# One sum of a seven-product group made by an accumulating DMA and used last, two more such groups per layer, and earlier chained sums, in a two-layer block on one Trainium2 core

## The chip, the cores and the metric

The kernel runs on one core of a Trainium2 chip. The metric is the device time of one execution in microseconds. The kernel before took 2232.99 us, the median of three runs (2231.83, 2232.99, 2235.12).

## What is computed

Two layers of a decoder act on 256 tokens of width 2048, in 32-bit floats. Each layer is a token mixer and then a SwiGLU feed-forward part; a last RMS norm follows.

```python
h = h + mixer(rmsnorm(h, w_mix))        # layer 0: gated delta rule and RG-LRU; layer 1: two attentions
h = h + swiglu(rmsnorm(h, ffn_norm[layer]), ffn_w_gate[layer], ffn_w_up[layer], ffn_w_down[layer])

def swiglu(hn, w_gate, w_up, w_down):
    return (jax.nn.silu(hn @ w_gate) * (hn @ w_up)) @ w_down
```

The gate and up matrices are 2048 x 5632, the down matrix is 5632 x 2048. The change lies in the feed-forward part, in the first weight products of layer 0, and in the last norm.

## The kernel before

**Split numbers.** A product in full float precision is made of three products of rounded numbers. A tile x is split into `hi`, x rounded to the matmul's format (a copy on ACT), and `lo` = x - hi (a subtraction on DVE). Then x·w is hi·hi + hi·lo + lo·hi: three matmuls. The activations X and hid lie in SBUF split already. Each weight tile of 128 x 1024 (512 KB) is loaded by SP's DMA queue into a `raw` buffer (`load`, L166; three buffers of one pool and four of another in the feed-forward part), and split by `split` (L176) into `whi` (four buffers) and `wlo` (three).

**Plain units.** A unit is one weight tile: two slices of 128 rows by 512 columns. It is multiplied with both halves of the tokens (t = 0, 1): 2 x 2 x 3 = 12 matmuls of 512 columns, into two of four PSUM banks F[t][i] (`Bank.add`, L399).

**Groups by sevens.** Four units (two row pairs u, two column blocks i) and the two token halves make a 2 x 2 by 2 x 2 block product. `seven` (L424) makes it of seven block products instead of eight, in Winograd's form of Strassen's scheme. Four sums of weight tiles are needed: T1 = b11 + b12, T2 = T1 + b22, T3 = b12 + b22, T4 = T2 + b21, whose signs are taken into the activations' sums and the results. `total` (L372) makes one sum on DVE into a `T` tile (three buffers) and splits it into the pair `thi` (ACT) and `tlo` (DVE), of which there are two buffers each. The sums of activations are made ahead by `combine` (L382), once per group of four X or hid slices, on DVE and ACT. A group has seven steps of six matmuls. Four products go to banks M[0] to M[3], the others straight to F; `ends` (L449) joins the M banks into four tiles e at the end. In order, the steps of the kernel before are: 1 b11; 2 T1; 3 b22; 4 T3; 5 T2; 6 b21; 7 T4.

**Blocks.** `block` (L409) runs the plain units of a block and puts the steps of its groups between them: the number of steps made after unit j grows by `len(sevens) / gaps`. In a block with 8 plain units and two groups (14 steps), three steps follow unit 1, four follow unit 2, three unit 3 and four unit 4: steps 4 to 7 of each group stand together. In a block with one group a plain unit stands between steps 5 and 6.

**The feed-forward part** (`ffn`, L482) goes through 11 gate blocks of 512 columns in pieces of 4, 4 and 3. A gate block is 16 units for X: four groups of four. `groups` says how many of these go by sevens: none in the first, two in each other. After each piece two down blocks (p = 0, 1) multiply the piece's hid with the rows of the down matrix. A down block after four gate blocks has four groups of four units, one of them by sevens. `hooks` are calls ahead of unit j: `turn` transposes the last block's results into hid, `late` combines hid[:, 0:4].

**Order.** The framework plans the order of each engine's instructions ahead of time. It takes what is ready by its own times, in the order of the program, so an engine's order can differ from that of the code. Each engine then works its list off in order, and waits for semaphores. A buffer of a tag is given again when its last reader is done.

**First products and last norm.** `first` (L210) loads the tokens and the first weights of layer 0 slice by slice and splits them, for u < 2 slice by slice, then two slices at a time. `second_half` (L1137) makes the last norm: per half of the rows two means (L1145), a root on ACT (L1147), a reciprocal, and the scalings (`ready`, L1155).

Of the kernel before, what the change touches and what calls it, by code (L numbers as in the profile page):

```python
# [4 lines left out]
F32, F32R, I32 = dt.float32, dt.float32r, dt.int32  # L5
AF = mybir.ActivationFunctionType
ALU = mybir.AluOpType
# [3 lines left out]
D = 2048  # L11
T = 256
NK = D // 128
# [34 lines left out]
def body(tc, A, out):  # L48
# [161 lines left out]
    def first(src, n, w):  # L210

        m = T + n * 128
        xw = [h.rearrange("p a b -> p (a b)")] + [ogp.tile([128, 4 * D // 2], F32, name=f"xw{i}", tag="og") for i in range(3)]
        xw = [t[:, 0:4 * m].rearrange("p (k n) -> p k n", n=m) for t in xw]
        Ps = [acc.tile([128, T], F32, name="Pw", tag="acc") for _ in range(n)]
        for a, b in [(k, k + 1) for k in range(4)] + [(k, k + 2) for k in range(4, NK, 2)]:
            nc.sync.dma_start(xw[a // 4][:, a % 4:a % 4 + b - a], src[:, a:b])  # L220
            if b == 12:
                nc.sync.dma_start(tab[:, 0:NTAB0], A["tab"][:, 0:NTAB0])
                nc.sync.dma_start(col[:, 16:], A["col"][:, 16:])
        for u in range(NK // 2):
            hi = wh.tile([128, 1024], F32R, name="whi")
            lo = wl.tile([128, 1024], F32R, name="wlo")
            for a, b in [(0, 1), (1, 2)] if u < 2 else [(0, 2)]:
                ks = range(2 * u + a, 2 * u + b)
                for k in ks:
                    x = xw[k // 4][:, k % 4, 0:T]  # L230
                    S.activation(X[:, k, 0], x, AF.Copy, scale=w[:, k:k + 1])
                    V.scalar_tensor_tensor(out=X[:, k, 1], in0=x, scalar=w[:, k:k + 1], in1=X[:, k, 0].bitcast(F32),
                                           op0=ALU.mult, op1=ALU.subtract)
                raw = xw[u // 2][:, u % 2 * 2 + a:u % 2 * 2 + b, T:]
                c = slice(512 * a, 512 * b)
                rows = lambda t: t[:, c].rearrange("p (k n) -> p k n", n=n * 128)
                if u == a == 0:
                    V.tensor_copy(rows(hi), raw)
                else:
                    S.copy(rows(hi), raw)  # L240
                V.tensor_sub(rows(lo), raw, rows(hi).bitcast(F32))
                for k in ks:
                    for i, P in enumerate(Ps):
                        ws = slice((k % 2 * n + i) * 128, (k % 2 * n + i + 1) * 128)
                        PE.matmul(P, hi[:, ws], X[:, k, 0], start=k == 0, stop=False)
                        PE.matmul(P, hi[:, ws], X[:, k, 1], start=False, stop=False)
                        PE.matmul(P, lo[:, ws], X[:, k, 0], start=False, stop=k == NK - 1)
            if u % 2:
                sq = xw[u // 2][:, :, 0:T]
                tc.keep_in_program_order(S.activation(sq, sq, AF.Square))  # L250
        return Ps, [t[:, :, 0:T] for t in xw]
# [60 lines left out]

    def sumsq(g, *ts):
        for t in ts or range(2):
            j = (mx.tile([128, 1024], F32, name="junk", tag="T", bufs=3)[:, 0:512] if more else
                 mx.tile([128, 512], F32, name="junk", tag="t2", bufs=4))
            S.activation(j, h[:, t, g * 512:(g + 1) * 512], AF.Square, accum_out=ssp[:, t, g:g + 1])

# [50 lines left out]
        return f  # L369


    def total(a, b, name):  # L372

        t = mx.tile([128, 1024], F32, name=name, tag="T", bufs=3)
        V.tensor_tensor(out=t, in0=a, in1=b, op=ALU.add)  # L375
        hi = fp.tile([128, 1024], F32R, name="thi", tag="thi", bufs=2)
        lo = fp.tile([128, 1024], F32R, name="tlo", tag="tlo", bufs=2)
        S.copy(hi, t)  # L378
        V.tensor_sub(lo, t, hi.bitcast(F32))  # L379
        return t, (hi, lo)  # L380

    def combine(x4):  # L382

        f = mx.tile([128, 4, T], F32, name="cf", tag="T", bufs=3)
        c = mx.tile([128, 4, 2, 128], F32, name="cc4", tag="T", bufs=3)
        r = fp.tile([128, 2, 4, 2, 128], F32R, name="comb", tag="comb", bufs=3)
        V.tensor_tensor(out=f, in0=x4[:, :, 0].bitcast(F32), in1=x4[:, :, 1].bitcast(F32), op=ALU.add)
        a11, a21, a12, a22 = (f[:, 2 * j:2 * j + 2, t * 128:(t + 1) * 128] for j in range(2) for t in range(2))
        for i, (x, y) in enumerate(((a21, a22), (a21, a11), (a22, c[:, 1]), (a12, c[:, 2]))):
            V.tensor_tensor(out=c[:, i], in0=x, in1=y, op=ALU.subtract)  # L390
        S.copy(r[:, 0], c)
        V.tensor_tensor(out=r[:, 1], in0=c, in1=r[:, 0].bitcast(F32), op=ALU.subtract)
        return r

    class Bank:
# [3 lines left out]
        def add(self, A, B):  # L399
# [6 lines left out]
                PE.matmul(self.t, xl, hi[:, kk], start=False, stop=kk == 1 and self.i == self.n - 1)  # L406
            self.i += 1

    def block(src, x, comb, nd, hooks, tail=0, lead=2, trail=None):  # L409


# [12 lines left out]
        def seven(m):  # L424
# [2 lines left out]
            q = lambda j, t: lambda kk: xs(4 * m + 2 * j + kk, t)  # L427
            b11 = load(src(0, 2 * m))
            M[0].add(q(0, 0), split(b11))
            yield  # L430
            b12 = load(src(1, 2 * m))
            t, w = total(b11, b12, "T1")
            M[1].add(cx(0), w)
            yield
            b22 = load(src(1, 2 * m + 1))
            F[0][1].add(cx(3), split(b22))
            yield
            M[3].add(cx(1), total(b12, b22, "T3")[1])
            yield
            t, w = total(t, b22, "T2")  # L440
            M[2].add(cx(2), w)
            yield
            b21 = load(src(0, 2 * m + 1))
            F[0][0].add(q(1, 0), split(b21))
            yield
            F[1][0].add(q(1, 1), total(t, b21, "T4")[1])
            yield

        def ends():  # L449
            c1, v, w5, w7 = (mx.tile([128, 512], F32, name=f"e{i}", tag=f"e{i}", bufs=1) for i in range(4))  # L450
            S.copy(c1, M[0].t)
            for o, a, b, op in ((v, M[2], c1, ALU.subtract), (w5, M[1], v, ALU.add), (v, M[3], v, ALU.add), (w7, M[3], w5, ALU.add)):
                V.tensor_tensor(out=o, in0=a.t, in1=b, op=op)
            return [[c1, w5], [v, w7]]
# [27 lines left out]
    def ffn(L, then, fin=None):  # L482
# [18 lines left out]
        for groups in ((0, 2, 2, 2), (2, 2, 2, 2), (2, 2, 2)):  # L501
# [3 lines left out]
            for j in range(piece):  # L505
# [3 lines left out]
                    hooks[8] = rstd  # L509
                    hooks[10] = lambda: cx.update({1: combine(X[:, 4:8])})  # L510
                if j == 1 and piece == 3:
                    hooks.update(late)
                F, e = block(lambda i, u: gu[b, u, i], lambda k: X[:, k], {m: lambda m=m: cx[m] for m in range(groups[j])}, 4, hooks)
                a = [fp.tile([128, 512], F32, name=f"fa{t}", tag="fa", bufs=2) for t in range(2)]
                for t in range(2):
                    if e:
                        V.tensor_tensor(out=a[t], in0=F[t][0], in1=e[t][0], op=(ALU.add, ALU.subtract)[t])
                    S.activation(a[t], a[t] if e else F[t][0], AF.Silu, scale=nrm["rs"][:, t:t + 1])
                for t in range(2):
                    if e:  # L520
                        V.tensor_tensor(out=e[t][1], in0=F[t][1], in1=e[t][1], op=ALU.add)
                    V.scalar_tensor_tensor(out=a[t], in0=e[t][1] if e else F[t][1], scalar=nrm["rs"][:, t:t + 1], in1=a[t],
                                           op0=ALU.mult, op1=ALU.mult)
                    todo.append((hid, j, t, a[t]))
                b += 1
            u0 = 2 * (b - piece)
            for p in range(2):
                end = b == NB and p == 1
                hooks = {2: turn} if todo else {}
                if p == 0 and piece == 4:  # L530
                    hooks.update(late)
                if end and fin:
                    hooks.update({5: lambda: then(0), 6: lambda: then(1)})
                last = (3, 1, 3) if end and fin else (0, 5 if 4 in hooks else 2)
                F, e = block(lambda i, u: dn[2 * p + i, u0 + u], lambda k: hid[:, k], {0: lambda: ch[0]}, piece, hooks, *last)
                hs = [[h[:, t, (2 * p + i) * 512:(2 * p + i + 1) * 512] for i in range(2)] for t in range(2)]
                for t in range(2):
                    for i in range(2):
# [598 lines left out]
    def second_half(add):  # L1137

        o = fo[0]
        x, y, z = ([f[:, t:t + 1] for t in range(2)] for f in (xf, yf, zf))  # L1140

        def root(t):

            for i, o in ((2, z[t]), (3, x[t])):
                V.scalar_tensor_tensor(out=o, in0=ssp[:, t, i:i + 1], scalar=1.0 / D, in1=part[:, t:t + 1] if i == 2 else z[t],  # L1145
                                       op0=ALU.mult, op1=ALU.add)
            S.activation(y[t], ssp[:, t, 3:4], AF.Sqrt, scale=1.0 / D, bias=z[t])  # L1147

        def rate(t):
# [15 lines left out]
        add(0, 1)  # L1165
        sumsq(3, 0)
        add(1, 0)
        root(0)
        sumsq(2, 1)
        rate(0)  # L1170
        ready(0, 0)
        add(1, 1)
        sumsq(3, 1)
        ready(0, 2)
        ready(0, 3)
        root(1)
        ready(0, 1)
        rate(1)
        for g in (0, 2, 1, 3):
# [97 lines left out]
```

## Time and profile before

| | before |
|---|---|
| median of three runs | 2232.99 us |
| the profiled execution's own time | 2232.51 us |
| its span, first to last instruction | 2230.7 us |
| matmuls recorded | 11026 |
| granted TensorE clock, mean | 0.999 |
| read from HBM | 418.22 MB |

PE is the engine of the matmuls, PEld its weight loads, DVE the vector engine, ACT the scalar engine, POOL the general one, SP the one that issues most DMAs; a name with q is an engine's queue. A line of a group gives line, engine, operation, the tile written and those read, shapes, count, then busy us and the mean ns of one, then the idle time before them and what ended it. A line in order of time begins with the start and the duration in us. A line of waits gives the total, the number and the longest. A line of a stretch gives for PE, PEld, DVE, ACT and POOL the busy us and the count, then the granted clock, the share of the 16 DMA engines and GB/s. Matmuls overlap, so the time of one is read from the distance of starts.

### The profile page before, as it was taken

How to read it: one execution, taken by the hardware profiler on the slowest of the kernel's cores; microseconds unless marked ns; L12 is line 12 of the kernel's file. 1: busy time of each engine (PE TensorE's matmuls, PEld its weight loads, DVE VectorE, ACT ScalarE, POOL GpSimd, SP SyncE). 2: the span in 40 equal slices, each digit the busy share in tenths (PEclk: the TensorE clock that was granted, in tenths of full speed). 3: DMA queues.
4: the chain of work that ended last, by engine and by line, in shares of the span. 5: the costliest groups of instructions: out<-in, count | busy, mean ns of one | idle time of the engine just before them, and what ended most of it. 6: DMA issues, size and time to landing. Idle time of an engine off the chain costs nothing.

```text
span 2230.7 us, 30096 instructions
## 1 busy us (share of the span) xinstructions
PE 2215.9 (99%) x11026; PEld 1852.0 (83%) x11026; DVE 1928.9 (86%) x2716; ACT 1278.9 (57%) x1670; POOL 2.1 (0%) x6
## 2 busy tenths in 40 slices
PE   9999999999999999999999999999999999999998
PEld 8888888888888888888878888888888888888886
DVE  8899676789989999899966658857999999999998
ACT  6776664565555665565654444445665466555565
POOL 0000000000000000000000000000000000000000
PEclk9999999999999999999999999999999999999999
DMA  7445445665565666656545455456665666666563
GB/s 280 161 144 168 140 150 187 214 208 195 192 215 196 201 195 203 207 187 200 180 158 175 158 172 172 162 186 217 208 198 191 208 205 203 194 210 202 181 219 131
DMA packets 117780, 422.29 MB, mean 189 GB/s; under 512 B 13152, under 2 KB 14688, under 8 KB 117504
## 3 DMA queue, kind: packets, MB, share of 16 engines
q1 hardware_dynamic: 117344, 420.10, 56.7%
q8 instruction: 86, 1.41, 0.2%
q14 instruction: 62, 0.51, 0.1%
q10 hardware_dynamic: 288, 0.27, 0.0%
HBM read 418.22 MB, written 2.10 MB: 188 GB/s over the span
## 4 chain that ended last, share of the span: by engine, by line
PE 97%; DVE 1%; DMA 1%; ACT 0%; issue 0%; SPq 0%; DVEq 0%; ACTq 0%
PE F L405 16%; PE F L406 16%; PE F L404 16%; PE Pw L199 11%; PE Pw L204 6%; PE Px L303 5%; PE Px L305 5%; PE Px L304 5%; PE M L404 4%; PE M L405 4%; PE M L406 4%; PE Ph L492 1%; PE Psc L1053 1%; PE Pt L326 0%; PE Ps L563 0%; DMA raw<-in_gu 0%
## 5 line engine op out<-in xcount | busy, mean ns | idle before, releaser
L179 ACT CAST whi<-raw 128x1024 fp32r<-128x1024 f32 x724 | 760.7, 1052 | 744.8 <-PE F L406 359.1
L180 DVE TENSOR_TENSOR wlo<-raw,whi 128x1024 fp32r<-128x1024 f32 x724 | 876.5, 1219 | 185.0 <-PE Px L304 74.0
L199 PE MATMUL Pw<-X,whi 128*128 128x512 f32 x1088 | 388.0, 400 | 0.0
L404 PE MATMUL F<-whi,X 128*128 128x512 f32 x848 | 330.5, 391 | 0.0
L405 PE MATMUL F<-wlo,X 128*128 128x512 f32 x848 | 330.4, 390 | 0.0
L406 PE MATMUL F<-whi,X 128*128 128x512 f32 x848 | 330.1, 389 | 0.0
L204 PE MATMUL Pw<-X,wlo 128*128 128x256 f32 x1088 | 304.7, 280 | 0.1
L378 ACT CAST thi<-T 128x1024 fp32r<-128x1024 f32 x208 | 219.1, 1054 | 98.6 <-DVE T L375 71.5
L379 DVE TENSOR_TENSOR tlo<-T,thi 128x1024 fp32r<-128x1024 f32 x208 | 252.5, 1219 | 24.7 <-ACT thi L378 24.2
L199 PEld LDWEIGHTS Pw<-X,whi 128*128 128x128 f32 x1088 | 204.1, 188 | 47.4 <-issue 0.5
L405 PE MATMUL F<-wlo,hid 128*128 128x512 f32 x536 | 208.9, 390 | 0.0
L406 PE MATMUL F<-whi,hid 128*128 128x512 f32 x536 | 208.7, 389 | 0.0
L404 PE MATMUL F<-whi,hid 128*128 128x512 f32 x536 | 208.6, 390 | 0.0
L204 PEld LDWEIGHTS Pw<-X,wlo 128*128 128x128 f32 x1088 | 205.4, 189 | 1.2 <-DVE wlo L180 0.7
L406 PEld LDWEIGHTS F<-whi,X 128*128 128x128 f32 x848 | 159.2, 188 | 33.1
L404 PEld LDWEIGHTS F<-whi,X 128*128 128x128 f32 x848 | 159.2, 188 | 32.7
L405 PEld LDWEIGHTS F<-wlo,X 128*128 128x128 f32 x848 | 159.3, 188 | 32.5
L375 DVE TENSOR_TENSOR T<-raw,raw 128x1024 f32<-128x1024 f32 x98 | 119.2, 1218 | 11.0 <-DMA raw<-in_gu 8.9
L375 DVE TENSOR_TENSOR T<-T,raw 128x1024 f32<-128x1024 f32 x104 | 126.6, 1218 | 1.9 <-DMA raw<-in_dn 1.7
L404 PE MATMUL M<-thi,comb 128*128 128x512 f32 x312 | 121.3, 391 | 0.6 <-ACT thi L378 0.6
L405 PE MATMUL M<-tlo,comb 128*128 128x512 f32 x312 | 121.6, 390 | 0.0
L406 PE MATMUL M<-thi,comb 128*128 128x512 f32 x312 | 121.5, 389 | 0.0
(385 smaller groups left out, 3217.1 us busy)
## 6 DMA issues: line engine op xcount, KB each, us to landing
raw<-in_gu SPq DMA_DIRECT2D x352, 512.0 KB, 4.1
raw<-in_dn SPq DMA_DIRECT2D x176, 512.0 KB, 4.3
raw<-in_w0w SPq DMA_DIRECT2D x72, 512.0 KB, 3.6
raw<-in_wo SPq DMA_DIRECT2D x64, 512.0 KB, 3.5
raw<-in_w1w SPq DMA_DIRECT2D x64, 512.0 KB, 3.6
raw<-in_w1x SPq DMA_DIRECT2D x32, 512.0 KB, 3.6
raw<-in_w0x SPq DMA_DIRECT2D x16, 512.0 KB, 3.6
xw<-in_xw SPq DMA_DIRECT2D x6, 768.0 KB, 10.9
```

The source lines that it names most:

```text
L179: S.copy(hi, raw)
L180: V.tensor_sub(lo, raw, hi.bitcast(F32))
L199: PE.matmul(P.rearrange("p a b -> p (a b)"), hi[:, kk], X[:, k].rearrange("p a b -> p (a b)"), start=k == 0, stop=False)
L204: PE.matmul(P[:, 0], lo[:, kk], X[:, k, 0], start=False, stop=k == NK - 1)
L303: PE.matmul(Ps[t], x[:, 0, ts], hi[:, kk], start=k == 0, stop=False)
L304: PE.matmul(Ps[t], x[:, 0, ts], lo[:, kk], start=False, stop=False)
L375: V.tensor_tensor(out=t, in0=a, in1=b, op=ALU.add)
L378: S.copy(hi, t)
L379: V.tensor_sub(lo, t, hi.bitcast(F32))
L404: PE.matmul(self.t, xh, hi[:, kk], start=self.i == kk == 0, stop=False)
L405: PE.matmul(self.t, xh, lo[:, kk], start=False, stop=False)
L406: PE.matmul(self.t, xl, hi[:, kk], start=False, stop=kk == 1 and self.i == self.n - 1)
```

## The change

- In `seven`, T3 is no longer made on DVE: once T1 has been summed, POOL issues a DMA that loads b22 a second time and adds it onto b12 in SBUF. T3 is used last. The order of steps is now: 1 b11; 2 b22; 3 T1; 4 b21; 5 T2; 6 T4; 7 T3.
- T1, T2 and T4 are made in one tile, in place, each right behind the split of the sum before it, a step ahead of its own split. `total` becomes `halves`, which only splits. The tag `T` has two buffers in place of three.
- In the down blocks p = 1 of pieces with four gate blocks, hid's second group of four goes by sevens too; its `combine` is made ahead of unit 9 of the down block p = 0. `comb` has four buffers in place of three.
- The tiles e take the place of the tiles `fa` in the gate blocks.
- In the third piece, `late` is called ahead of unit 6 of its second block and no longer ahead of unit 4.
- In `first`, slices 4 and 5 are loaded and split one by one.
- In `second_half`, the two means are made in calls of their own: the first stands ahead of the scalings of the other half, the second behind the root.

```diff
-        for a, b in [(k, k + 1) for k in range(4)] + [(k, k + 2) for k in range(4, NK, 2)]:
+        for a, b in [(k, k + 1) for k in range(6)] + [(k, k + 2) for k in range(6, NK, 2)]:
...
-            for a, b in [(0, 1), (1, 2)] if u < 2 else [(0, 2)]:
+            for a, b in [(0, 1), (1, 2)] if u < 3 else [(0, 2)]:
...
-    def total(a, b, name):
-
-        t = mx.tile([128, 1024], F32, name=name, tag="T", bufs=3)
-        V.tensor_tensor(out=t, in0=a, in1=b, op=ALU.add)
+    def halves(t):
+
         hi = fp.tile([128, 1024], F32R, name="thi", tag="thi", bufs=2)
         lo = fp.tile([128, 1024], F32R, name="tlo", tag="tlo", bufs=2)
         S.copy(hi, t)
         V.tensor_sub(lo, t, hi.bitcast(F32))
-        return t, (hi, lo)
+        return hi, lo
...
-        r = fp.tile([128, 2, 4, 2, 128], F32R, name="comb", tag="comb", bufs=3)
+        r = fp.tile([128, 2, 4, 2, 128], F32R, name="comb", tag="comb", bufs=4)
...
             b11 = load(src(0, 2 * m))
             M[0].add(q(0, 0), split(b11))
-            yield
             b12 = load(src(1, 2 * m))
-            t, w = total(b11, b12, "T1")
-            M[1].add(cx(0), w)
+
+            t = mx.tile([128, 1024], F32, name="T", tag="T", bufs=2)
+            more_of = lambda a, b: V.tensor_tensor(out=t, in0=a, in1=b, op=ALU.add)
+            more_of(b11, b12)
+
+            G.dma_start(b12, src(1, 2 * m + 1), accum_op=ALU.add)
             yield
             b22 = load(src(1, 2 * m + 1))
             F[0][1].add(cx(3), split(b22))
             yield
-            M[3].add(cx(1), total(b12, b22, "T3")[1])
-            yield
-            t, w = total(t, b22, "T2")
-            M[2].add(cx(2), w)
+            M[1].add(cx(0), halves(t))
+            more_of(t, b22)
             yield
             b21 = load(src(0, 2 * m + 1))
             F[0][0].add(q(1, 0), split(b21))
             yield
-            F[1][0].add(q(1, 1), total(t, b21, "T4")[1])
+            M[2].add(cx(2), halves(t))
+            more_of(t, b21)
+            yield
+            F[1][0].add(q(1, 1), halves(t))
+            yield
+            M[3].add(cx(1), halves(b12))
             yield
...
-                    hooks.update(late)
+
+                    hooks[6] = late[4]
...
+                    hooks[9] = lambda hid=hid: ch.update({1: combine(hid[:, 4:8])})
...
-                F, e = block(lambda i, u: dn[2 * p + i, u0 + u], lambda k: hid[:, k], {0: lambda: ch[0]}, piece, hooks, *last)
+                F, e = block(lambda i, u: dn[2 * p + i, u0 + u], lambda k: hid[:, k],
+                             {m: lambda m=m: ch[m] for m in range(1 + (p == 1 and piece == 4))}, piece, hooks, *last)
...
+        def mean(t, i):
+
+            V.scalar_tensor_tensor(out=(z, x)[i][t], in0=ssp[:, t, 2 + i:3 + i], scalar=1.0 / D,
+                                   in1=z[t] if i else part[:, t:t + 1], op0=ALU.mult, op1=ALU.add)
+
         def root(t):
...
-            for i, o in ((2, z[t]), (3, x[t])):
-                V.scalar_tensor_tensor(out=o, in0=ssp[:, t, i:i + 1], scalar=1.0 / D, in1=part[:, t:t + 1] if i == 2 else z[t],
-                                       op0=ALU.mult, op1=ALU.add)
```

More of the change, by code (lines that the diff above doesn't have):

```diff
@@ L314, in sumsq @@
         for t in ts or range(2):
-            j = (mx.tile([128, 1024], F32, name="junk", tag="T", bufs=3)[:, 0:512] if more else
+            j = (mx.tile([128, 1024], F32, name="junk", tag="T", bufs=2)[:, 0:512] if more else
                  mx.tile([128, 512], F32, name="junk", tag="t2", bufs=4))
@@ L379, in total @@
         V.tensor_sub(lo, t, hi.bitcast(F32))
-        return t, (hi, lo)
+        return hi, lo
     def combine(x4):
-        f = mx.tile([128, 4, T], F32, name="cf", tag="T", bufs=3)
-        c = mx.tile([128, 4, 2, 128], F32, name="cc4", tag="T", bufs=3)
-        r = fp.tile([128, 2, 4, 2, 128], F32R, name="comb", tag="comb", bufs=3)
+        f = mx.tile([128, 4, T], F32, name="cf", tag="T", bufs=2)
+        c = mx.tile([128, 4, 2, 128], F32, name="cc4", tag="T", bufs=2)
+        r = fp.tile([128, 2, 4, 2, 128], F32R, name="comb", tag="comb", bufs=4)
         V.tensor_tensor(out=f, in0=x4[:, :, 0].bitcast(F32), in1=x4[:, :, 1].bitcast(F32), op=ALU.add)
@@ L407, in add, with sums @@
             self.i += 1
+    def sums():
+        return [[mx.tile([128, 512], F32, name=f"e{t}{i}", tag=f"e{t}{i}", bufs=1) for i in range(2)] for t in range(2)]
     def block(src, x, comb, nd, hooks, tail=0, lead=2, trail=None):
@@ L445, in seven @@
             yield
-            F[1][0].add(q(1, 1), total(t, b21, "T4")[1])
+            M[2].add(cx(2), halves(t))
[4 more added lines that the diff above has]
+            M[3].add(cx(1), halves(b12))
             yield
         def ends():
-            c1, v, w5, w7 = (mx.tile([128, 512], F32, name=f"e{i}", tag=f"e{i}", bufs=1) for i in range(4))
+            (c1, w5), (v, w7) = sums()
             S.copy(c1, M[0].t)
@@ L511, in ffn @@
                 if j == 1 and piece == 3:
-                    hooks.update(late)
+                    hooks[6] = late[4]
                 F, e = block(lambda i, u: gu[b, u, i], lambda k: X[:, k], {m: lambda m=m: cx[m] for m in range(groups[j])}, 4, hooks)
-                a = [fp.tile([128, 512], F32, name=f"fa{t}", tag="fa", bufs=2) for t in range(2)]
+                a = e or sums()
                 for t in range(2):
                     if e:
-                        V.tensor_tensor(out=a[t], in0=F[t][0], in1=e[t][0], op=(ALU.add, ALU.subtract)[t])
-                    S.activation(a[t], a[t] if e else F[t][0], AF.Silu, scale=nrm["rs"][:, t:t + 1])
+                        V.tensor_tensor(out=a[t][0], in0=F[t][0], in1=e[t][0], op=(ALU.add, ALU.subtract)[t])
+                    S.activation(a[t][0], a[t][0] if e else F[t][0], AF.Silu, scale=nrm["rs"][:, t:t + 1])
                 for t in range(2):
                     if e:
[L521 to L524, printed above, removed]
+                        V.tensor_tensor(out=a[t][1], in0=F[t][1], in1=e[t][1], op=ALU.add)
+                    V.scalar_tensor_tensor(out=a[t][0], in0=a[t][1] if e else F[t][1], scalar=nrm["rs"][:, t:t + 1],
+                                           in1=a[t][0], op0=ALU.mult, op1=ALU.mult)
+                    todo.append((hid, j, t, a[t][0]))
                 b += 1
@@ L1167, in second_half @@
         add(1, 0)
+        mean(0, 0)
         root(0)
+        mean(0, 1)
         sumsq(2, 1)
@@ L1173, in second_half @@
         sumsq(3, 1)
+        mean(1, 0)
         ready(0, 2)
@@ L1176, in second_half @@
         root(1)
+        mean(1, 1)
         ready(0, 1)
```

## The prediction

> **What bounds the kernel now.** I read the page's head and chain first, then PE's waits, then the groups, one feed-forward stretch in time order, and last the DMA rows.
>
> ```profile
> span 2230.7 us, 30096 instructions
> ...
> PE 2215.9 (99%) x11026; PEld 1852.0 (83%) x11026; DVE 1928.9 (86%) x2716; ACT 1278.9 (57%) x1670; POOL 2.1 (0%) x6
> ...
> PE 97%; DVE 1%; DMA 1%; ACT 0%; issue 0%; SPq 0%; DVEq 0%; ACTq 0%
> ```
> ```profile
> PE Pz L93 <- ACT tab L90: 2.7, 1, 2.7
> PE Pw L245 <- ACT whi L240: 0.7, 1, 0.7
> PE Pgate L645 <- ACT cx L582: 0.6, 1, 0.6
> PE M L404 <- ACT thi L378: 0.6, 1, 0.6
> PE F L405 <- DVE tlo L379: 0.4, 1, 0.4
> ```
> The chain that ended last is PE, and all of PE's listed waits come to 5.0 us, 1.0 of it in the feed-forward parts. So time is worth what matmuls are worth, as long as nobody makes PE wait. What a matmul is worth is not the 390 ns that its row shows, because matmuls overlap; it is the distance between starts:
>
> ```profile
> 699.71 0.39 PE L404 MATMUL M<-thi,comb 128*128 128x512 f32 x1
> ...
> 701.07 0.39 PE L404 MATMUL F<-whi,X 128*128 128x512 f32 x1
> ...
> 702.43 0.39 PE L404 MATMUL F<-thi,X 128*128 128x512 f32 x1
> 702.66 0.39 PE L405 MATMUL F<-tlo,X 128*128 128x512 f32 x1
> ...
> 703.79 0.39 PE L404 MATMUL F<-whi,X 128*128 128x512 f32 x1
> ...
> 706.51 0.39 PE L404 MATMUL M<-whi,X 128*128 128x512 f32 x1
> ```
> These are steps 5, 6 and 7 of a group by sevens, then a plain unit. Six matmuls take 1.36 us, so one takes 0.227, and twelve 2.72. The second engine is nearly as full:
>
> ```profile
> 510.00:552.00 42.00, 42.00 (x190) 34.60 (x189) 41.60 (x43) 25.52 (x27) 0.00 (x0) 1.00 0.59 201
> ```
> In this 42-us stretch (one gate block) DVE is busy 41.6 us (the column after PE's and PEld's), ACT 25.5, the DMA engines 0.59, at full PE clock.
>
> **Part 1, two more groups by sevens per stage.** A plain group of four tiles is 48 matmuls, a group by sevens 42.
>
> ```profile
> L404 PE MATMUL M<-thi,comb 128*128 128x512 f32 x312 | 121.3, 391 | 0.6 <-ACT thi L378 0.6
> L378 ACT CAST thi<-T 128x1024 fp32r<-128x1024 f32 x208 | 219.1, 1054 | 98.6 <-DVE T L375 71.5 <-PE M L406 23.6 <-PE F L406 1.8
> ```
> 312 at six per group, or 208 sums at four, make 52 groups. The edit adds one in the p = 1 down block of each of the two four-block pieces of each of two layers: 4 groups, 24 matmuls, 24 x 0.227 = **-5.4 us**. PE does these inside its bound, so it counts in full if DVE follows.
>
> **Part 2, DVE.** Successive 1.22-us operations on DVE start 1.14 apart (702.26 and 703.40 below). Each group loses one of four sums: a gate block has two groups and falls by 2.3 of its 41.6 us. The changed down block goes from 23 large operations to 28 (8 units, twice 10): 28 x 1.14 + 12 small at 0.61 (717.14 to 717.75) = 39.2, under PE's 180 x 0.227 = 40.9. The block ahead of it gets one more `combine`:
>
> ```profile
> L390 DVE TENSOR_TENSOR cc<-cf,cc 128x256 f32<-128x256 f32 x20 | 8.3, 417 | 0.0
> L392 DVE TENSOR_TENSOR comb<-cc,comb 128x1024 fp32r<-128x1024 f32 x10 | 12.2, 1220 | 0.3
> ```
> ```profile
> 485.18 0.87 PE Ph L492 x8
> ```
> ```profile
> 717.14 0.68 DVE L453 TENSOR_TENSOR e<-M,e 128x512 f32<-128x512 f32 x1
> 717.75 1.22 DVE L180 TENSOR_TENSOR wlo<-raw,whi 128x1024 fp32r<-128x1024 f32 x1
> ```
> Its sum is as large as the last row's: 1.22 + 4 x 0.42 + 1.22 = 4.1 us. There 22 x 1.14 + 2 x 4.1 + 14 x 0.61 = 41.8 stands against PE's 186 x 0.227 + 0.9 of transposes = 43.1 (the 0.87 is the row of Ph). Hidden by 1.3 us; were that cover gone, each us would land on PE four times. Cost 0. ACT, at 25.5 of 42, gets three casts more per new group and has room. The new POOL transfer waits for DVE's first sum alone, and nothing else is queued on POOL (2.1 us in all).
>
> **Part 3, the sum that DMA makes.** b12 += b22 leaves DVE for an accumulating transfer that POOL issues, 56 in all; no row shows one. Its nearest row is a plain load of the same 512 KB:
>
> ```profile
> q1 hardware_dynamic: 117344, 420.10, 56.7%
> raw<-in_gu SPq DMA_DIRECT2D x352, 512.0 KB, 4.1
> ACT whi L179 <- DMA raw<-in_gu: 16.7, 8, 4.5
> 675.65 1.22 DVE L375 TENSOR_TENSOR T<-raw,raw 128x1024 f32<-128x1024 f32 x1
> ```
> Landing takes 4.1 us; I bound the new one by 4.1 and by twice that. It has far more: the last row is the first sum of the group whose steps 5 to 7 are shown above. DVE ended it at 676.9, the transfer may go then, and its split has to be there for step 7, not before step 5 ends at 701.07 (Part 4). That is 24 us of cover; past it every us would cost each group a us. Engine time: 0.567 x 2230.7 us for 420.10 MB is 1.58 us per load; two transfers per 41.7-us block (180 x 0.227 and 0.9 of transposes) at 1.58 to 3.16 raise the share from 0.59 to 0.67 or 0.74. They'd fill the engines only at (1 - 0.59) x 41.7 / 2 = 8.5 us each. The raw buffers stay seven, and one of them is held longer; but with 352 gate loads issued a cast waited for one only 8 times, 16.7 us in all and none of it in PE's list, so I take 0. The Trainium skill ("Collectives: The Full Stack", The bandwidth ceiling) says that an add in the DMA engine costs because it reads two sources, not because it adds. By it the estimate is the 3.16 end, and the sum stays.
>
> **Part 4, three pairs in a row.** This is the step I distrust. The split pairs `thi`/`tlo` have two buffers. Before, a group uses them in steps 2, 4, 5, 7; now in 3, 5, 6, 7. So step 7's pair takes step 5's buffer, with only step 6 between. What that chain lasts is in step 7's pair before, which took step 4's:
>
> ```profile
> 699.91 1.05 ACT L378 CAST thi<-T 128x1024 fp32r<-128x1024 f32 x1 [0.30 <-PE M L406]
> 701.00 1.23 DVE L379 TENSOR_TENSOR tlo<-T,thi 128x1024 fp32r<-128x1024 f32 x1 [0.81 <-ACT thi L378]
> 702.26 1.23 DVE L375 TENSOR_TENSOR T<-T,raw 128x1024 f32<-128x1024 f32 x1
> 703.40 1.22 DVE L379 TENSOR_TENSOR tlo<-T,thi 128x1024 fp32r<-128x1024 f32 x1
> ```
> Step 4 ended at 699.71, `tlo` at 702.23: 2.52 us, and PE wanted it at 702.66, two steps and one matmul later (2.95). With one step between, PE wants it after 1.36 + 0.23 = 1.59: late by 0.93, with the handover (0.05) 0.98 us. Steps 4 to 7 stand together, without a plain unit between, in all groups of blocks with two groups: 40 gate + 8 down = 48. Price if PE keeps the order: 48 x 0.98 = +47 us. But the planner doesn't keep it where an operand is late:
>
> ```profile
> 1038.73 0.50 PE L404 MATMUL F<-thi,X 128*128 128x512 f32 x1
> 1039.07 0.40 PE L405 MATMUL F<-wlo,X 128*128 128x512 f32 x1
> ...
> 1041.40 0.39 PE L405 MATMUL F<-tlo,X 128*128 128x512 f32 x1
> ```
> Here step 7's first matmul runs, its `tlo` isn't there, and matmuls of the next plain unit fill 2.3 us before step 7 goes on. The next unit (2.72 us, ready long before) covers 0.98 easily. What is left is the seam: 1038.73 to 1039.07 is 0.34 instead of 0.23, a gap of 0.11. Bounds: 0 to 48 x 0.11 = 5.3; below zero isn't possible, as nothing here removes work. Most seams of such stretches have none, so I take one in five: **+1.1**.
>
> **Part 5, the chained sums one step ahead.** ACT's 71.5 us of waiting for DVE's T (row of L378) shrink, but ACT isn't the bound. Of PE's two feed-forward waits, 0.4 for `tlo` and 0.6 for `thi`, I take the first, whose engine gets room: **-0.4** (bounds 0 and -1.0).
>
> **Part 6, start and end.** The third weight pair is now split by halves.
>
> ```profile
> 12.12 0.38 PE L245 MATMUL Pw<-X,whi 128*128 128x256 f32 x1 [0.65 <-ACT whi L240]
> ...
> 13.05 0.28 PE L246 MATMUL Pw<-X,whi 128*128 128x256 f32 x1
> 13.38 0.74 PE L247 MATMUL Pw<-X,wlo 128*128 128x256 f32 x4
> ```
> PE waited 0.65 for the whole cast, then 13.38 - 13.05 - 0.12 = 0.21 for the difference; half-size operations come early enough for both: **-0.9**, bounds 0 (a later DVE wait takes it back) and -1.1. At the end the first mean of the second row block goes ahead of two scalings:
>
> ```profile
> 2223.34 0.29 ACT L1147 ACTIVATE fin<-ssp,fin 128x1 f32<-128x1 f32 x1 [0.73 <-DVE fin L1145]
> 2223.67 0.16 DVE L1151 RECIPROCAL fin<-fin 128x1 f32<-128x1 f32 x1 [0.15 <-ACT fin L1147]
> ```
> The root no longer waits 0.73, but DVE still has the two scalings and the other mean: **-0.2** (0 to -0.3).
>
> **Sum.** -5.4 + 1.1 - 0.4 - 0.9 - 0.2 = -5.8. The profiled execution took 2232.5 us (the span and 1.8 around it), 0.5 under the median of the three runs. 2232.5 - 5.8 = **2226.7 us**, or 0.26% less. A measurement of this kernel can tell about 0.2%, 4.5 us, from no change.
>
> **Rivals.**
> *Seams everywhere* (0.17): every step 7 pays its 0.11, +4.2 on the forecast: 2230.9, no change. For it: `thi` is ready 1.3 us after step 5, step 6 lasts 1.36, so just in time. Against: most filled steps show none.
> *Step 7 waits* (0.10, slower): PE keeps the order and Part 4's +47 less 1.1 gives 2272.6. It decides from 6.9 / 48 = 0.14 us of wait per group, which eats all the gain. For it: 2.52 against 1.59. Against: the fill at 1038.73.
> *The transfer is dear* (0.10, slower): at 10 us of all engines each, a block of 16 loads needs 25.3 + 20 = 45.3 us instead of 41.7; 28 such blocks give +101, 2328; from 8.5 on it costs. Against: a load takes 1.58.
> *POOL and DVE get in each other's way* (0.05): if each issue holds DVE for one operation, 1.22, a block gets 2.4 back of the 2.3 it gained, and the changed down blocks, with 1.7 spare, lose 0.7 each: 2230 to 2237. The Trainium skill ("SBUF — State Buffer", Who interferes with whom) has a DVE instruction with two SBUF inputs contend with GpSimd's reads; no run here shows it yet.
> *Forecast* (0.58), its own range 2223 to 2229.5.
>
> Range: 2222.5 to 2237 leaves out the two slower rivals, 0.20. Faster by over 0.2% (under 2228.5): nearly all of the forecast, 0.54. Within: the first and last rival and the forecast's edge, 0.25. Slower: 0.21.
>
> **What would show it.** 24 fewer matmuls; 56 issues on POOL landing within 10 us; on PE's rows the last five matmuls of step 7 behind matmuls of a plain unit; DVE about 38 of 42 in a gate block; DMA share 0.67 to 0.74; PE's list of waits still short. A wait of M for `tlo` or `thi` some 48 times, about 1 us each, would make me wrong by Part 4; a wait of `thi` for a DMA, by Part 3.

## The result, and the profile after

The changed kernel takes **2241.6 us** (median of 6 runs, 2240.13 to 2242.65), the kernel before 2233.59 us (6 runs in the same comparison, 2231.83 to 2235.12): a ratio of 1.0035, 95% interval 1.0025 to 1.0045. It is 8.0 us slower where 5.8 us faster was forecast, and above the range of 2222.5 to 2237.

First the head of the page, its chain, and PE's list of waits (total us, times, longest).

```profile
span 2238.3 us, 30376 instructions
...
PE 2219.2 (99%) x11002; PEld 1842.3 (82%) x11002; DVE 1919.4 (86%) x2713; ACT 1289.9 (58%) x1687; POOL 50.6 (2%) x62
...
PE 92%; DVE 4%; DMA 2%; issue 1%; ACT 1%; DVEq 0%; ACTq 0%; SPq 0%
```
```profile
PE M L403 <- DVE tlo L377: 6.0, 9, 1.3
PE Pz L93 <- ACT tab L90: 2.7, 1, 2.7
PE Pgate L657 <- ACT cx L594: 0.6, 1, 0.6
...
```

The 24 matmuls are gone (11002 of 11026). Yet the chain leaves PE in 8% of the span instead of 3, and the list has a new first line: M, waiting for `tlo`. Here is the same by groups, the three matmul forms of M that use a split sum (busy us, mean ns of one, idle us before), and behind them two of these forms in the kernel before:

```profile
L403 PE MATMUL M<-tlo,comb 128*128 128x512 f32 x336 | 134.6, 401 | 6.3 <-DVE tlo L377 6.0
L402 PE MATMUL M<-thi,comb 128*128 128x512 f32 x336 | 134.1, 399 | 0.0
L404 PE MATMUL M<-thi,comb 128*128 128x512 f32 x336 | 131.1, 390 | 0.0
```
```profile
L405 PE MATMUL M<-tlo,comb 128*128 128x512 f32 x312 | 121.6, 390 | 0.0
L406 PE MATMUL M<-thi,comb 128*128 128x512 f32 x312 | 121.5, 389 | 0.0
```

The first two were 390 and 391 ns before and are now 401 and 399, while the third went from 389 to 390. 336 x (11 + 8) ns is 6.4 us, and with 6.3 us of idle time it makes 12.7. That is nearly all there is to explain: from their first matmul to their last, the two feed-forward parts last 4.2 and 4.0 us longer than before although they lost 5.4 us of matmuls, so 13.6 us came in. Outside them the first part starts 0.2 later, and the tail behind the last matmul is 0.9 shorter.

One group in order of time, PE first, then ACT and DVE beside it:

```profile
702.20 0.39 PE L404 MATMUL M<-thi,comb 128*128 128x512 f32 x1
702.42 0.40 PE L402 MATMUL F<-thi,X 128*128 128x512 f32 x1
...
703.59 0.39 PE L404 MATMUL F<-thi,X 128*128 128x512 f32 x1
703.81 0.46 PE L402 MATMUL M<-thi,comb 128*128 128x512 f32 x1
704.11 0.39 PE L402 MATMUL F<-whi,X 128*128 128x512 f32 x1
...
704.81 0.39 PE L402 MATMUL F<-whi,X 128*128 128x512 f32 x1
705.03 0.50 PE L403 MATMUL M<-tlo,comb 128*128 128x512 f32 x1
705.37 0.40 PE L404 MATMUL M<-thi,comb 128*128 128x512 f32 x1
```
```profile
702.67 1.05 ACT L376 CAST thi<-raw 128x1024 fp32r<-128x1024 f32 x1 [2.48 <-PE M L404]
```
```profile
703.75 1.22 DVE L377 TENSOR_TENSOR tlo<-raw,thi 128x1024 fp32r<-128x1024 f32 x1 [1.30 <-ACT thi L376]
```

Step 5 ends with the matmul of 702.20. Only then may ACT cast into its pair, and ACT had stood idle for it. The cast ends at 703.72, and step 7's first matmul starts at 703.81; the next follows after 0.30 instead of 0.227. `tlo` ends at 704.97, step 7 goes on at 705.03, and the next follows after 0.34. So the plan does put plain matmuls between, as forecast, but both operands come at the very last moment, and that costs 0.07 and 0.11. Counted over the trace, 48 of M's `thi` matmuls last over 0.42 us, as many as there are groups in blocks with two groups, and 36 of its `tlo` matmuls; before it was 5 and 2. All of them are step 7's. Each of the 48 starts 0.05 to 0.11 us behind the cast that it needs, and 42 of these casts had been held by a matmul of M, as the one above; none had been held by a load.

With no slack, whatever else DVE has to do lands on PE. Here is `tlo` of another such step, on DVE and then on PE:

```profile
831.36 1.22 DVE L385 TENSOR_TENSOR cf<-hid 128x1024 f32<-128x1024 f32 x1
832.50 1.22 DVE L377 TENSOR_TENSOR tlo<-raw,thi 128x1024 fp32r<-128x1024 f32 x1
```
```profile
832.06 0.40 PE L404 MATMUL F<-whi,X 128*128 128x512 f32 x1
833.77 0.50 PE L403 MATMUL M<-tlo,comb 128*128 128x512 f32 x1 [1.31 <-DVE tlo L377]
```

A sum of `combine` stands ahead of it on DVE, and PE stops for 1.31 us. In ten of PE's twelve stops ahead of such a matmul, 4.9 of the 6.3 us, it is the next group's first sum, which itself had waited on DVE for a load, 0.4 to 1.6 us; the longest are behind 678.2, 1607.6 and 2072.1, where PE loses 0.9 to 1.5.

The other steps' rows: the DMA queues and issues (last column: median us to landing), and the gate block shown before as 41.60 busy on DVE and 0.59 of the DMA engines.

```profile
q1 hardware_dynamic: 117488, 420.10, 58.1%
q0 software_dynamic: 8064, 29.36, 7.9%
...
raw<-in_gu SPq DMA_DIRECT2D x352, 512.0 KB, 4.4
...
raw<-in_gu POOLq DMA_DIRECT2D x40, 512.0 KB, 6.5
...
raw<-in_dn POOLq DMA_DIRECT2D x16, 512.0 KB, 7.3
```
```profile
511.20:552.90 41.70, 41.70 (x188) 34.11 (x187) 38.71 (x40) 24.44 (x26) 0.86 (x1) 1.00 0.75 223
```

56 transfers, landing in 6.5 and 7.3 us (medians of the two rows), DVE at 38.7 of 41.7, and a DMA share of 0.75: the transfers and DVE behave as forecast.

### The profile page after: what moved, and what is told of

Its sections match the earlier page's. It is cut to its first block, busy times and chain, and to the rows that moved or that the text cites. A ratio compares the mean times of both kernels' runs of the same rounds, so it can differ in the third digit from the quotient of the medians.

```text
span 2238.3 us, 30376 instructions
## 1 busy us (share of the span) xinstructions
PE 2219.2 (99%) x11002; PEld 1842.3 (82%) x11002; DVE 1919.4 (86%) x2713; ACT 1289.9 (58%) x1687; POOL 50.6 (2%) x62
## 4 chain that ended last, share of the span: by engine, by line
PE 92%; DVE 4%; DMA 2%; issue 1%; ACT 1%; DVEq 0%; ACTq 0%; SPq 0%
PE F L404 15%; PE F L403 15%; PE F L402 15%; PE Pw L199 10%; PE Pw L204 5%; PE Px L303 5%; PE Px L305 5%; PE Px L304 5%; PE M L403 4%; PE M L402 4%; PE M L404 4%; DMA raw<-in_gu 2%; DVE wlo L180 1%; DVE tlo L377 1%; PE Ph L500 1%
## 5 line engine op out<-in xcount | busy, mean ns | idle before, releaser
L199 PE MATMUL Pw<-X,whi 128*128 128x512 f32 x1088 | 388.1, 400 | 0.0
L376 ACT CAST thi<-T 128x1024 fp32r<-128x1024 f32 x168 | 176.7, 1052 | 141.6 <-DVE T L435 117.2
L199 PEld LDWEIGHTS Pw<-X,whi 128*128 128x128 f32 x1088 | 204.2, 188 | 47.5 <-issue 0.5
L377 DVE TENSOR_TENSOR tlo<-T,thi 128x1024 fp32r<-128x1024 f32 x168 | 205.0, 1220 | 18.1 <-ACT thi L376 15.9
L402 PE MATMUL F<-whi,hid 128*128 128x512 f32 x480 | 187.6, 391 | 0.0
L404 PE MATMUL F<-whi,hid 128*128 128x512 f32 x480 | 187.0, 390 | 0.0
L403 PE MATMUL F<-wlo,hid 128*128 128x512 f32 x480 | 186.9, 389 | 0.0
L435 DVE TENSOR_TENSOR T<-T,raw 128x1024 f32<-128x1024 f32 x112 | 136.6, 1219 | 5.5 <-DMA raw<-in_gu 4.6
L403 PE MATMUL M<-tlo,comb 128*128 128x512 f32 x336 | 134.6, 401 | 6.3 <-DVE tlo L377 6.0
L402 PE MATMUL M<-thi,comb 128*128 128x512 f32 x336 | 134.1, 399 | 0.0
L404 PE MATMUL M<-thi,comb 128*128 128x512 f32 x336 | 131.1, 390 | 0.0
L404 PEld LDWEIGHTS F<-whi,hid 128*128 128x128 f32 x480 | 90.1, 188 | 18.9
```

Source lines behind the costliest of these rows:

```text
L199: PE.matmul(P.rearrange("p a b -> p (a b)"), hi[:, kk], X[:, k].rearrange("p a b -> p (a b)"), start=k == 0, stop=False)
L402: PE.matmul(self.t, xh, hi[:, kk], start=self.i == kk == 0, stop=False)
L403: PE.matmul(self.t, xh, lo[:, kk], start=False, stop=False)
L435: more_of = lambda a, b: V.tensor_tensor(out=t, in0=a, in1=b, op=ALU.add)
```

## Experiments

**Theory A**: step 7's pair comes too late, because with two pairs it has to take the one that step 5 leaves, and only step 6 lies between. **Theory B**: the accumulating transfer costs, by its landing or by what it does to the loads beside it. **Theory C**: the second groups in the down blocks load DVE too much. **Theory D** came up during the runs: what matters is when raw buffers come free and loads go out. All times below are medians of 4 to 11 runs; ratios are against the kernel before, run beside them.

**e1, another order of the steps.** The pairs alternate with steps of plain weights:
```
 b11, T1, b22, T2, b21, T4, T3      (changed kernel: b11, b22, T1, b21, T2, T4, T3)
```


> The changed kernel with the seven steps of a group in another order: b11, T1, b22, T2, b21, T4, T3. A step that uses a split sum now has a step of plain weights behind it, and the last step's pair is the one that step 4 left, with steps 5 and 6 between; number of matmuls, sums, transfers and second groups are those of the changed kernel. Theory A (step 7's pair is late because it takes the pair of step 5): PE's waits of M for tlo, 24 us on the page of after, all but go, the feed-forward stretches lose 10 to 14 us of gaps, time 2226 to 2231 us. Theory B (the accumulating transfer, by its landing or by contention): no change, 2239 to 2243 us. Theory C (the second groups in the down blocks load DVE too much): no change either, 2239 to 2243 us.

Measured: **2227.93 us**, ratio 0.9975 (0.9964 to 0.9985). That is below both kernels. The same two matmul forms:
```profile
L403 PE MATMUL M<-tlo,comb 128*128 128x512 f32 x336 | 131.7, 392 | 1.1 <-DVE tlo L377 0.6
L402 PE MATMUL M<-thi,comb 128*128 128x512 f32 x336 | 131.3, 391 | 0.0
```
They are back at 392 and 391 ns, the idle time fell from 6.3 to 1.1. (The 24 us of waits in the expectation were 6.0 of PE's and 18.1 of its weight loads', PEld.) B and C are out as causes of the 8 us, since neither the transfers nor the second groups were touched.

**e9, one move alone.** Steps 4 and 5 of the changed kernel change places; nothing else:
```
-            b21 = load(src(0, 2 * m + 1))
-            F[0][0].add(q(1, 0), split(b21))
-            yield
             M[2].add(cx(2), halves(t))
+            b21 = load(src(0, 2 * m + 1))
             more_of(t, b21)
             yield
+            F[0][0].add(q(1, 0), split(b21))
+            yield
             F[1][0].add(q(1, 1), halves(t))
```


> The changed kernel with one move: steps 4 and 5 change places (b11, b22, T1, T2, b21, T4, T3), so that two steps, not one, lie between the step that leaves a pair and step 7 that takes it; everything else is the changed kernel. Theory A: most of what e1 won comes with this one move, 2227 to 2233 us. Theory D (e1 won because its loads come at other times): no change to half of it, 2236 to 2243 us.

Measured: 2229.84 us, ratio 0.9982 (0.9973 to 0.9991). From 1.0035 this is 0.0053, or 11.8 us, from one step more between the step that leaves a pair and the step that takes it. The rows:
```profile
L403 PE MATMUL M<-tlo,comb 128*128 128x512 f32 x336 | 131.8, 392 | 1.6 <-DVE tlo L377 1.6
L402 PE MATMUL M<-thi,comb 128*128 128x512 f32 x336 | 131.2, 390 | 0.2 <-ACT thi L376 0.2
```
The time came back in the very matmuls that theory A names. The run alone doesn't exclude D, because the load of b21 now stands behind T2's split, and T4's sum a step earlier. In the changed kernel's trace the 48 late matmuls are A's: the pair held 42 of their casts, a load none. In ten of the stops a late load has a part.

**e10, T4 right behind T2**, on the pair that T1 left: b11, T1, b22, T2, T4, b21, T3.


> The order b11, T1, b22, T2, T4, b21, T3: T4 right behind T2, on the pair that T1 left at step 2; step 7 has steps 5 and 6 between as in e1. Theory A: as e1, 2225 to 2231 us. If T4's own sum (T2's sum plus b21, whose load must now be there a step sooner) comes late: 2232 us or more, with waits of F for thi or tlo.

Measured: 2231.11 us, ratio 0.9983 (0.9975 to 0.9992), at the upper edge of what A allowed. With the transfer and T3 last, the three orders with two steps ahead of step 7 are all faster than the kernel before, and the one with a single step is slower. This run also tells A from D in the stops: here first sums still wait 11.7 us on DVE for loads (14.4 in the changed kernel, 8.8 in the one before; waits over 0.3 us), yet M waits only 1.1 for `tlo`. A late load costs PE where the pair leaves no slack.

**e3, without the second groups in the down blocks**, and **e4, the same with three pairs**, whose room is the combine buffer that those groups needed:
```
-                             {m: lambda m=m: ch[m] for m in range(1 + (p == 1 and piece == 4))}, ...
+                             {m: lambda m=m: ch[m] for m in range(1)}, ...
```
```
-        hi = fp.tile([128, 1024], F32R, name="thi", tag="thi", bufs=2)
+        hi = fp.tile([128, 1024], F32R, name="thi", tag="thi", bufs=3)     # tlo as well
```


> The changed kernel without the second group by sevens in the four down blocks, and without their combine: 24 matmuls more, 5.4 us of PE. Theory A: 8 dense groups of 48 lose their late step 7 with the edit (8 x 0.2 to 0.3 us = about 2 us), so 2241.6 + 5.4 - 2 = 2244 to 2247 us. Theory C (the down groups cost more than they save): faster than the changed kernel, 2237 us or less. Theory B says 2246 to 2247 us.

> As the kernel without the second down groups, with three buffers for the split pairs in place of two (room for it comes from a combine buffer that these down groups needed); order of steps as in the changed kernel. Theory A: step 7's pair takes step 3's buffer and can be made before step 6; 8 to 12 us faster than the kernel without the second down groups, about 2233 to 2238 us, and M's waits for tlo below 5 us. Theory B: no change against that kernel, 2244 to 2247 us.

Measured: e3 2262.19 us (1.0126, 1.0112 to 1.0140), e4 2233.92 us (0.9998, 0.9989 to 1.0007). A third pair, in the changed order of steps, is worth 28 us, and PE's waits of M for `tlo` are gone from e4's list. That is A's direction, at almost three times its size, and e3 is 15 us above what any theory gave. It isn't faster, as C would have it, but it doesn't test C cleanly either, since it brings a loss of its own that is not seams. PE, then ACT:
```profile
703.76 0.39 PE L404 MATMUL F<-thi,X 128*128 128x512 f32 x1
708.10 0.79 PE L402 MATMUL M<-thi,comb 128*128 128x512 f32 x1 [3.95 <-ACT thi L376]
708.69 0.63 PE L402 MATMUL F<-whi,X 128*128 128x512 f32 x1
709.12 0.63 PE L403 MATMUL F<-wlo,X 128*128 128x512 f32 x1
```
```profile
705.11 1.99 ACT L179 CAST whi<-raw 128x1024 fp32r<-128x1024 f32 x2 [6.67 <-DMA raw<-in_gu]
707.01 1.04 ACT L376 CAST thi<-raw 128x1024 fp32r<-128x1024 f32 x1
```
The cast of step 7 stands on ACT behind two casts of plain weights, and these waited 6.67 us for a load. When PE goes on, matmuls last 0.63 and start 0.43 apart. Three such stops (704, 964, 1813), with the slow matmuls behind each, cost 17 us.

**e7, nine raw buffers in e3**, from the same room, and **e8, e3 with the sum on VectorE:**
```
-        if more and loads[0] > 0 and loads[0] % 7 in (1, 3, 5, 6):
-            raw = mx.tile([128, 1024], F32, name="raw4", tag="raw4", bufs=4)
+        if more and loads[0] > 0 and loads[0] % 9 in (1, 3, 4, 5, 7, 8):
+            raw = mx.tile([128, 1024], F32, name="raw4", tag="raw4", bufs=6)
```
```
-            G.dma_start(b12, src(1, 2 * m + 1), accum_op=ALU.add)
             yield
             b22 = load(src(1, 2 * m + 1))
+            V.tensor_tensor(out=b12, in0=b12, in1=b22, op=ALU.add)
```


> As e3 (changed order, two pairs, no second down groups), with nine buffers for the loaded weights in place of seven; the room is the combine buffer that gave e4 its third pair. Theory A (the pair): no better than e3, 2255 to 2263 us. Theory D (in e3 the loads come late because sums that wait for their step hold two of the seven buffers; a cast of plain weights was 6.7 us late for a load, and the cast of the last sum stands behind it): most of e3's four waits of 4 us go, 2240 to 2250 us.

> As e3, with b12 += b22 on VectorE in place of the transfer. Theory A: no better than e3, 2255 to 2263 us. Theory B (the transfer slows the loads that go beside it, 6.7 us to landing in place of 4.3): loads land in about 4.2 us again, the four long waits go, 2240 to 2250 us.

Measured: e7 2245.93 us (1.0053, 1.0040 to 1.0065), e8 2251.98 us (1.0080, 1.0066 to 1.0093). Two more raw buffers recover 16 of e3's 28 us, and the long stops are gone: PE's longest wait in the feed-forward parts is 1.4. Without the transfer 10 us come back, and loads land in 4.1 again. So in e3 several things meet: a sum that waits for its pair keeps its raw buffer, the next loads go out late, ahead of the stop at 704 they take 6.7 us to land beside a transfer, and the cast that PE needs is queued behind them. Each of the three remedies (pair, buffers, no transfer) helps for itself. D is right for e3; the pair is the larger lever.

**e2, the sum on VectorE in the changed kernel** (same edit as e8, with the second groups).


> The changed kernel with b12 += b22 made on VectorE behind the load of b22, in place of the accumulating transfer on POOL: 56 transfers fewer, 56 sums of 1.14 us on DVE more; order of steps as in the changed kernel. Theory B (the transfer costs): the time falls by 4 us or more, to 2237 us or less. Theory A: the pair chain stays, and DVE has 64 us more to do; same or slower, 2240 to 2255 us, with the waits of M for tlo as large as before or larger.

Measured: 2241.60 us, ratio 1.0038 (1.0024 to 1.0052), the same as the changed kernel. The loss only changed its place:
```profile
PE F L403 <- DVE wlo L180: 6.5, 3, 3.1
PE Pz L93 <- ACT tab L90: 2.7, 1, 2.7
PE M L403 <- DVE tlo L377: 1.8, 2, 1.4
```
M waits 1.8 instead of 6.0, against my expectation, since the plan around step 7 comes out differently; F waits 6.5 for `wlo`, nearly all of it in one stop of 3.1 us per layer, which e5 shows below. Taken alone, this run would have said that the transfer is worth nothing.

**e5, the same in e1's order**, and **e12, in the step order of before** (b11, T1, b22, T3, T2, b21, T4).


> The reordered kernel of e1 with b12 += b22 made on VectorE behind the load of b22, in place of the accumulating transfer. Theory A (the order of the pairs alone decides, the transfer is neither cost nor need): within 3 us of e1, 2226 to 2231 us, DVE's busy time up by about 56 x 1.0 us. Rival (DVE needs the relief that the transfer gives: with the sum back, a gate block has 41.6 us of work in 41.7 again and a changed down block 40.3 of 40.9): 2232 us or more, with waits of F for wlo.

> The step order of the kernel before and b12 += b22 on VectorE, no transfer: what remains of the change are the four second groups, the chained sums a step ahead and the edits at start and end. If DVE has no room without the transfer (as e5): 2237 to 2243 us, waits of F for wlo in the blocks with two groups. If the groups are worth their matmuls by themselves: 2225 to 2230 us.

Measured: e5 2241.36 us (1.0033, 1.0021 to 1.0045), 13 us above e1; e12 2247.68 us (1.0061, 1.0048 to 1.0074), above both of its ranges. A alone would have had e5 at e1's time: the order isn't enough. The same stretch as above, in e5:
```profile
511.20:552.90 41.70, 41.70 (x189) 34.56 (x188) 41.31 (x44) 24.98 (x27) 0.00 (x0) 1.00 0.64 206
```
DVE is busy 41.31 of 41.70, about as full as before the change, and yet PE loses nothing in this block. The loss lies at one place per layer. PE, then DVE:
```profile
1021.78 1.00 PE L402 MATMUL F<-whi,X 128*128 128x512 f32 x3
1025.87 0.50 PE L403 MATMUL F<-wlo,X 128*128 128x512 f32 x1 [3.09 <-DVE wlo L180]
```
```profile
1022.14 1.22 DVE L390 TENSOR_TENSOR comb<-cc,comb 128x1024 fp32r<-128x1024 f32 x1
1023.27 1.41 DVE L531 SCALAR_TENSOR_TENSOR e<-e,rs,e 128x512 f32<-128x512 f32 x2
1024.59 3.49 DVE L180 TENSOR_TENSOR wlo<-raw,whi 128x1024 fp32r<-128x1024 f32 x3
```
The `wlo` that PE needs stands behind the end of a `combine` and the last operations of a gate block. This is the third piece's `combine`, which the change calls ahead of unit 6 and no longer ahead of unit 4. With the slow matmuls behind it the stop costs 5.0 us, and so does the one at 2122: 10 of the 13 us. e2 and e12 have the same two stops of 3.09 us. In the kernel before, DVE is just as full from 1005 to 1028 (22.81 us of 23.00, 22.93 in e5), but its `combine` has ended by 1005.6, and PE doesn't stop. So the transfer is worth 13 us here mostly because it keeps this spot clear; whether the earlier call would have done so without it, no run shows. Order and transfer make a square of four: changed order 2241.6 with and without the transfer, e1's order 2227.9 with it and 2241.4 without.

**e6, e1 without the second down groups** (edit as in e3).


> The reordered kernel of e1 without the second groups in the four down blocks: 24 matmuls more. If these groups are worth their matmuls once the order is right: e1 + 5.4 us, 2232 to 2235 us. If they cost something else besides: less than that. If e3's 20 us come from leaving them out, and not from the late pair: 2245 us or more.

Measured: 2246.77 us, ratio 1.0059 (1.0046 to 1.0071): 18.8 us above e1, of which 5.4 are the matmuls. The other 13.4 are two stops like e3's, of 4.0 and 4.4 us, which cost 14.7 with the wait and the slow matmuls behind them; here is the first:
```profile
704.92 0.39 PE L404 MATMUL F<-thi,X 128*128 128x512 f32 x1
709.27 0.80 PE L402 MATMUL M<-thi,comb 128*128 128x512 f32 x1 [3.96 <-ACT thi L376]
710.52 0.80 PE L403 MATMUL M<-tlo,comb 128*128 128x512 f32 x1 [0.46 <-DVE tlo L377]
```
Why the plan without these groups runs into that stop, in the first gate block behind the down blocks, and the plan with them doesn't, stays open; the planner lays all the work behind an edit anew.

**e11, T3 early with the transfer kept**: the step order of before, b12's sum still made by the transfer.


> The step order of the kernel before (b11, T1, b22, T3, T2, b21, T4) with the accumulating transfer kept: T3's split is wanted two or three steps behind T1 and no longer at the end; the raw buffer of b12 comes free three steps sooner. If the transfer needs its cover (about 7 us to landing, then 1.05 for the cast and 1.2 for the difference, against about 4 us of steps): 15 to 28 of the 56 groups wait 2 to 4 us each unless plain units fill in, 2245 to 2300 us. If the planner fills that, and the held buffer was what cost: 2226 us or less.

Measured: 2302.15 us, ratio 1.0304 (1.0290 to 1.0318). ACT's list names it:
```profile
ACT thi L376 <- DMA raw<-in_gu: 78.1, 25, 6.5
...
ACT thi L376 <- DMA raw<-in_dn: 63.6, 16, 7.2
```
41 of 56 casts wait for the transfer, 3.5 us on average (141.7 / 41); the total is just above the range I gave. The transfer is free only with T3 at the end, and at the end T3 needs a pair that is free early.

## Why the prediction was wrong

- **What bounds it**: right. Nearly every us was found on PE, by the distance of starts.
- **Part 1** (24 matmuls, -5.4): right; 11002 matmuls.
- **Part 2** (DVE has room): right for the kernel as changed, 38.71 busy in 41.7. Without the transfer e5 is 13 us slower, 10 of them in two stops behind one `combine` per layer.
- **Part 3** (transfer, cost 0): right in the changed kernel. 0.079 x 2238.3 / 56 gives 3.16 us of all engines per transfer, twice a load's 1.58, the upper of the two bounds. The Trainium skill ("Collectives: The Full Stack", The bandwidth ceiling) names two source reads as the cost of such an add; the trace agrees with the estimate made from it. The cover of about 24 us is real: e11 takes it away and pays 60 us more than the changed kernel. What I had not seen is that some loads beside a transfer land late: of the 215 that were in flight beside one, a tenth took over 6.6 us, up to 8.9, although their median is 4.5, against 4.3 for the others. Where a kernel has less slack (e3), they are felt.
- **Part 4: here it failed.** The chain (2.52 us against 1.59) and the fill by plain matmuls were right, the price of the fill was not: the term of +1.1 was too small. I took one seam of 0.11 in five groups, +1.1. What came: step 7's `thi` just in time in 48 groups and its `tlo` in 36, 6.4 us in the two mean durations, and 6.3 us of waits, which I had at none because a unit of 2.72 us covers 0.98. The cover is there, but it is cover for DVE in order, too: an operation of 0.7 to 1.2 us ahead of `tlo`, or one that waits for a load, uses it up. +12.7 instead of +1.1 is 11.6 of the 13.8 us by which the forecast missed; about 1 us more came into the feed-forward parts and isn't placed. 12.7 / 48 is 0.26 us per group, over the 0.14 at which the second rival decides; its mechanism was right in a weaker form, the order wasn't kept and the wait came all the same.
- **Part 5** (-0.4): the two waits it named are gone from the list, and F's matmuls with `tlo` fell from 396 to 390 ns; right, and lost in Part 4.
- **Part 6** (-0.9 and -0.2): the matmuls behind the changed start (L199) begin at 29.12 instead of 29.79, and by the first feed-forward matmul that is lost again (431.16, 430.95 before): +0.2 in place of -0.9, past the bound of 0. The tail is 0.9 shorter, more than the -0.3 that was its bound.
- **Rivals**: the first one, seams everywhere, came true with the reason that it gave (a cast ready just in time): 6.4 us in the two mean durations, where it had 1.1 + 4.2. It lacked the 6.3 us of waits. The contention of POOL and DVE isn't seen; a sum on DVE lasts 1.22 us before and after.
- With one step moved (e9), the forecast's sum comes out within its interval: -4.0 us there, -5.6 in e1, against -5.8.

## What to carry to other kernels

When steps are put in another order, count for each rotating buffer how many steps lie between the one that leaves it and the one that takes it next, and compare with the time that refilling lasts; "the planner fills it" is a price, not zero, as everything queued ahead of the late operand now lands on PE. Free the slot early (one step moved gave 11.8 us) before judging the rest of a change. And where DVE, buffers and order are all near their limits, test edits in pairs: the transfer was worth nothing in one order and 13 us in the other, and most of the 13 fell where a third edit had moved a `combine`.

## What the runs showed of the hardware

**A stop of PE can cost more than its length.** e12, clock granted (the number ahead of the last two) in four stretches; PE stood from 1024.7 to 1027.8:
```profile
1020.00:1024.30 4.30, 4.30 (x21) 3.34 (x19) 3.92 (x8) 3.53 (x5) 0.00 (x0) 1.00 0.40 122
1024.30:1027.90 3.60, 0.51 (x3) 0.20 (x2) 3.60 (x5) 0.65 (x1) 0.00 (x0) 0.89 0.00 0
1027.90:1028.50 0.60, 0.60 (x2) 0.50 (x3) 0.60 (x1) 0.00 (x0) 0.00 (x0) 0.50 0.00 0
1028.50:1033.50 5.00, 5.00 (x13) 3.88 (x12) 3.90 (x4) 0.96 (x2) 0.00 (x0) 0.50 0.76 246
```
Behind 3.1 us of standing still the clock is 0.50, and matmuls start 0.43 apart for another 6.1 us (2.7 behind e3's stop at 704). In the feed-forward parts of all these runs the granted clock falls to 0.50 for 3.4 or 6.8 us at a time. The Trainium skill ("TensorE: Matmul & The Clock Gate", What's actually happening) has the clock halved after an idle window of about 3.4 us that runs freely, and released after a busy one. The two levels and the 3.4 us agree with the traces; but a stop could be shorter than that window here. Of 21 stops of 1.8 us or more, 18 brought the half clock (one of 2.3 us in e8) and 3 did not (one of 3.1 us in e2). Shorter stops, all of the changed kernel's feed-forward parts among them, brought none.

**A matmul whose operand has just come** lasts 0.46 to 0.50 instead of 0.39, and the next starts 0.07 to 0.11 late; the list of waits doesn't count this. What in the engine costs it, the runs don't show.

**An accumulating transfer** of 512 KB into SBUF took 3.16 us of all DMA engines and landed in 6.5 and 7.3 us (medians, gate and down matrix), against 1.58 (kernel before) and 4.4 for a load.
